# A hybrid encoder layer on one core: the second attention branch loads split queries, keys and masked biases instead of raw ones

## The chip, the cores and the metric

The kernel runs on one core of a Trainium2 chip. The metric is the device time of one execution in microseconds (us). TensorE (PE) multiplies matrices into PSUM, with its weight loads (PEld) beside it; VectorE (DVE), ScalarE (ACT) and GpSimd (POOL) work element by element; SyncE (SP) issues most DMAs.

## What is computed

A sandwich-normalised encoder layer on 1024 sample and 256 prompt positions of width 1024, each a request of its own:

```python
h = rms_norm(x, pre_mix_norm)
qa, ka, va, qb, kb, vb, g_a, g_b = jnp.split(h @ w_in, SPLIT_POINTS, axis=-1)
o_a = gqa_branch(qa, ka, va, q_norm, k_norm) @ w_proj_a      # 8 query heads, 2 kv heads of 64
o_b = neighbourhood_branch(qb, kb, vb, rpb) @ w_proj_b       # 8 heads of 64
mix = (sigmoid(g_a + b) * o_a + sigmoid(g_b + b) * o_b) @ w_out
x = x + rms_norm(mix, post_mix_norm)
# channel mixer: up-projection, depthwise conv of 3, gelu(gate) * value, down-projection, norm, add
```

In the neighbourhood branch the positions are a grid of rows of 64 columns. A query sees 8 rows of 16 columns, each score gets a bias from a table of 15 x 31 per head (`rpb`), and the rest of the row is masked with minus infinity:

```python
s = einsum('bqhd,bwkhd->bhqwk', q_row, k_band) * scale + bias
s = where(col_mask, s, -inf); p = softmax(s, axis=(-2, -1))
```

All is float32. TensorE multiplies in a reduced form, so each operand x is held as two halves, hi = x rounded to that form and lo = x - hi, and a product takes two or three matmuls.

## The kernel before, in words

Splitting is a helper, `split_hi_lo` (L67): ScalarE casts hi (L68), VectorE subtracts lo (L69). A framework orders the instructions of each engine by a simulated timeline, in about the order in which the code states them, and sets the semaphores; `issue_after` and `behind` pin an instruction behind another on its engine. Each engine, SP's DMA queue too, then works in that fixed order.

1. First projections (to 178 us): for ten tiles of 128 positions the queries and keys of branch A with norms and rotary embedding (`project`, `rope`, `rope_t`). `rope_t` transposes and ScalarE copies the queries into the SBUF tile `qT` (L271). A second loop (L338) gives the values of both branches; between its steps `bias_tables` (L322) builds in DRAM the padded tables `rp_d` and `gv_d` of the relative bias, and the values of branch B go to DRAM by 64 stores (L355, on SP and ScalarE).

2. Branch A (178 to some 498 us): eight heads of five blocks of 256 queries. `Pipe.unit` interleaves the scores of a block with the transposes of the block before it and the outputs of the one before that. `q_stack` (L149) splits the queries of a head out of `qT`, two blocks ahead. At the second head the table `rq_d` for the prompt bias is written (L525). Softmax is a maximum on VectorE (L489), an exponential on ScalarE (L451), a reciprocal on VectorE (L453) and a normalisation on GpSimd (L454); the transposed probabilities are split (L68, L69).

3. Beside this, TensorE is filled with the rest of the projection (`fill_units`, L380): 24 blocks of 128 columns of `w_in`, 4 for the queries of branch B, 4 for its keys, 16 for the gates, each in three chunks of 512, 512 and 256 positions. A chunk is 24 matmuls (L395 to L397) in 8 units into one PSUM bank, `fp`, with `bufs=1`; then ScalarE copies the bank to the tile `fo`, scaling queries (L401), and SP stores it to `qb_d`, `kb_d` or `g_d` (L402). `fill_plan` and `fill` spread the units over the blocks: 216 of 576 in branch A, 32 at its end, up to 544 in branch B, the rest after. The 24 chunks of queries and keys are the first 192 units.

4. Branch B (some 500 to 780 us): eight heads of five blocks, four of 16 columns of the grid and one prompt block. `prep` (L555) loads the raw queries and keys of the next head, the bias `g16` in eight DMAs (L567), the values and the prompt bias `gp`; then, a step at a time between the blocks, ScalarE and VectorE split the keys (L589) and the queries, put into block order (L592 to L596), and GpSimd adds the row mask to the bias (L600) and the column mask to the prompt bias (L604). Scores: two matmuls (L620, L621), then one VectorE instruction that adds the bias and takes the maximum (L624). `sum_halves` (L456) adds the two halves of an output: ScalarE L458, VectorE L465, GpSimd L466.

5. From some 800 us: output projections, mix, and the channel mixer to 1893 us.

Of the kernel before, what the change touches and what calls it, by code (L numbers as in the profile page):

```python
# [16 lines left out]
P = 128  # L17
# [22 lines left out]
def encoder_layer_kernel(  # L40
# [52 lines left out]
    qb_d = scratch("qb_d", [4, P, NT])  # L93
    kb_d = scratch("kb_d", [4, P, NT])
# [8 lines left out]
    gv_d = scratch("gv_d", [NH, 16, 3, 23, 32])  # L103

# [40 lines left out]
    qT = T(av, "qT", [P, 4, NT])  # L145
    kH = T(av, "kH", [P, 2, NT], F32R)
    kL = T(av, "kL", [P, 2, NT], F32R)

    def q_stack(h):  # L149
        qs = T(qsp[0], "qs", [P, NT], F32R, bufs=2)  # L150
        a = slice((h % 2) * HD, (h % 2) * HD + HD)
        b = slice((1 - h % 2) * HD, (1 - h % 2) * HD + HD)
        src = qT[a, h // 2, :]
        nc.scalar.copy(qs[a, :], src)
        nc.vector.tensor_sub(qs[b, :], src, f32(qs[a, :]))
        return qs

    qsp = [None]
    qs_next = {}

    with ExitStack() as st:
# [104 lines left out]
        def rope_t(tt, qr, kr):  # L266
# [4 lines left out]
            nc.scalar.copy(qT[:, :, cols], tq)  # L271
# [44 lines left out]
        nc.sync.dma_start(rpad[:, 16:47], rpb[0].rearrange("h d c -> d h c"))  # L316
        bm = T(spv, "bm", [P, 3, 32])
# [4 lines left out]
        def bias_tables(step):  # L322
            if step == 1:
# [3 lines left out]
                nc.sync.dma_start(rp_d[15 * NH * 992:15 * NH * 992 + 32], rpad[0:1, 0:32])  # L327
            elif step == 3:
# [50 lines left out]

    def fill_units():  # L380
        for blk in range(24):
            if blk < 8:
                c0 = 768 + blk * P
                dst = (qb_d if blk < 4 else kb_d)[blk % 4]
                scale = QSCALE if blk < 4 else 1.0
            else:
                c0 = 2304 + (blk - 8) * P
                dst = g_d[blk - 8]
                scale = 1.0
            hi, lo = stream_w([(slice(0, NK), w_cols(w_in, c0))], () if blk else [fill_state["dve"].ins])  # L390
            for (t0, n) in CHUNKS:
# [8 lines left out]
                fo = T(stream, "fo", [P, 512], bufs=2)  # L400
                nc.scalar.activation(fo[:, 0:n], fp[:, 0:n], AF.Copy, scale=scale)  # L401
                nc.sync.dma_start(dst[:, t0:t0 + n], fo[:, 0:n])  # L402
# [68 lines left out]
    with va_stack:  # L471
        with ExitStack() as st:
# [45 lines left out]
            rpad2 = T(sp, "rpad2", [NH * 7, 127])  # L518
            nc.gpsimd.memset(rpad2, 0.0)
            nc.sync.dma_start(rpad2[:, 48:79], rpb[0][:, 4:11, :])  # L520

            pipe = Pipe()
            for h in range(NH):
                if h == 1:
                    nc.sync.dma_start(rq_d, rpad2.unsqueeze(1).to_broadcast([NH * 7, GW, 127]))  # L525
                qs = qs_next.pop(h)
                for j in range(5):
# [10 lines left out]
    with ExitStack() as st:  # L538
# [4 lines left out]
        cm = T(sp, "cm", [P, GW])  # L543
        nc.sync.dma_start(cm, col_mask)
        rm = T(sp, "rm", [P, 2, 12])
        nc.sync.dma_start(rm, row_mask)

        def by_block(ap, reverse):
            step = ap.ap[-1][0]
            first, dr = (15 * GW, -GW) if reverse else (0, 16)  # L550
            db = 16 if reverse else 256
            return bass.AP(tensor=ap.tensor, offset=ap.offset + first * step,
                           ap=[list(ap.ap[0]), [db * step, 4], [dr * step, 16], [step, 16]])

        def prep(h, res):  # L555
            pr, r0 = h // 2, (h % 2) * HD
            qraw = T(sp, "qraw", [HD, NT], bufs=1)
            nc.sync.dma_start(qraw, qb_d[pr, r0:r0 + HD, :])
            kraw = T(sp, "kraw", [P, NT], bufs=1)
            for half in range(2):  # L560
                nc.sync.dma_start(kraw[half * HD:(half + 1) * HD, :], kb_d[pr, r0:r0 + HD, :])
            g16 = T(sp, "g16", [P, 3, 16, 32], bufs=1)
            gt = gv_d[h]
            for r8 in range(8):
                src = bass.AP(tensor=gt.tensor, offset=gt.offset + r8 * 32,
                              ap=[[3 * 23 * 32, 16], [23 * 32, 3], [1, 512]])
                nc.sync.dma_start(g16[r8 * 16:(r8 + 1) * 16].rearrange("p v a b -> p v (a b)"), src)  # L567
# [4 lines left out]
            gp = T(sp, "gp", [P, 6, GW], bufs=2)  # L572
            rq = rq_d[h * 7:h * 7 + 1]
            for half in range(2):
                src = bass.AP(tensor=rq.tensor, offset=rq.offset + (1 - half) * GW * 127 + 63,
                              ap=[[126, GW], [GW * 127, 6], [1, GW]])
                nc.sync.dma_start(gp[half * GW:(half + 1) * GW], src)
            qs = T(sp, "qs", [P, NT], F32R, bufs=2)
            kh = T(sp, "kh", [P, NT], F32R, bufs=2)
            kl = T(sp, "kl", [P, NT], F32R, bufs=2)  # L580
            gb = T(sp, "gb", [P, 2, 3, 12, 32], bufs=2)
            ost = T(sp, "ost", [HD, NT], bufs=1)
            res.extend((gb, gp, qs, kh, kl, vB, ost))
            yield
# [90 lines left out]
        for _ in prep(0, cur):  # L675
            pass
# [644 lines left out]
```

## Time and profile before

| | us |
|---|---|
| median of 3 runs (lowest to highest) | 1897.12 (1894.83 to 1897.34) |
| the profiled execution | 1895.24 |
| its span, first to last instruction | 1893.5 |
| TensorE busy, of that span | 1841.7 (97%) |
| VectorE, ScalarE, GpSimd busy | 1253.2, 862.7, 673.7 |
| TensorE's mean granted clock | 0.993 |

The profile is of one execution. Busy time of a matmul is modelled to its end, so a busy TensorE need not be at its peak. A row of a timeline gives start and duration in us, the engine, the line of the kernel, the operation, output<-inputs, the shape and a count; in brackets stands how long the engine was idle before it and which instruction ended that. A row by stage gives for each engine the busy us and (x) the instructions, then the granted clock as a share of full speed, the mean busy share of the 16 DMA engines, and GB/s.

### The profile page before, as it was taken

The page shows a single profiled execution, that of the slowest core. Times are in us where ns is not written, and L with a number is a line of the kernel's source. Part 1 is how long each engine was busy: PE and PEld are TensorE (multiplying, and loading weights), DVE is VectorE, ACT ScalarE, POOL GpSimd, SP SyncE. Part 2 cuts the span into 40 slices and gives each one's busy share as a digit, 9 for nine tenths or more (in the row PEclk, how much of TensorE's full clock was granted, in tenths as well). Part 3 has the DMA queues.
Part 4 walks back from the last instruction along what each step waited for, and adds up shares of the span by engine and source line. Part 5 has one row for each costly group of instructions (what it writes and reads, how often), then busy time and mean ns, then how long its engine had stood idle before and what let it go on. Part 6 is the DMA issues. An engine that isn't in the chain of part 4 may idle for free.

```text
span 1893.5 us, 27341 instructions
## 1 busy us (share of the span) xinstructions
PE 1841.7 (97%) x10048; PEld 1590.3 (84%) x10048; DVE 1253.2 (66%) x1872; ACT 862.7 (46%) x1535; POOL 673.7 (36%) x609
## 2 busy tenths in 40 slices
PE   7999999999989999999999999999999999899998
PEld 7998888888778888888888888888888888778886
DVE  6844667667456766355644778877777776768775
ACT  4322667566446555444432434444444443553332
POOL 3731322222155544102111355543334432166531
PEclk9999999999989999999999999999999999999999
DMA  5146411111485663364532212322222223798865
GB/s 192 34 110 204 82 37 47 44 40 48 116 192 159 161 157 107 94 209 149 187 120 91 69 63 79 102 93 79 76 80 94 91 86 107 257 307 268 268 208 178
DMA packets 237352, 240.74 MB, mean 127 GB/s; under 512 B 32737, under 2 KB 183201, under 8 KB 237089
## 3 DMA queue, kind: packets, MB, share of 16 engines
q1 hardware_dynamic: 235537, 234.52, 41.3%
q10 hardware_dynamic: 1680, 4.46, 0.7%
q8 instruction: 79, 1.29, 0.3%
q14 instruction: 56, 0.46, 0.1%
HBM read 169.38 MB, written 69.55 MB: 126 GB/s over the span
## 4 chain that ended last, share of the span: by engine, by line
PE 63%; DVE 3%; DMA 2%; issue 2%; POOL 1%; ACT 1%; DVEq 0%; POOLq 0%; ACTq 0%; SPq 0%
PE pp L804 10%; PE pp L805 10%; PE pp L803 10%; PE big L744 5%; PE sml L805 3%; PE sml L804 3%; PE sml L803 3%; PE fp L395 2%; PE fp L396 2%; PE fp L397 2%; PE big L767 2%; PE big L765 2%; PE big L766 2%; DMA wr<-in_w_down_dram 2%; PE sml L744 1%
## 5 line engine op out<-in xcount | busy, mean ns | idle before, releaser
L454 POOL TENSOR_SCALAR p<-p,rs 128x384 f32<-128x384 f32 (+2 forms) x160 | 130.4, 818 | 303.4 <-DVE rs L453 259.2
L395 PE MATMUL fp<-bigH,fh 128*128 128x512 f32 (+1 forms) x544 | 207.7, 382 | 6.3 <-ACT fo L401 5.3
L397 PE MATMUL fp<-bigH,fl 128*128 128x512 f32 (+1 forms) x544 | 195.9, 360 | 0.5 <-DVE fl L69 0.5
L396 PE MATMUL fp<-bigL,fh 128*128 128x512 f32 (+1 forms) x544 | 196.0, 360 | 0.0
L804 PE MATMUL pp<-bigL,th 128*128 128x512 f32 (+1 forms) x556 | 192.4, 346 | 0.0
L803 PE MATMUL pp<-bigH,th 128*128 128x512 f32 (+1 forms) x556 | 191.9, 346 | 0.0
L805 PE MATMUL pp<-bigH,tl 128*128 128x512 f32 (+1 forms) x556 | 190.7, 346 | 0.0
L1115 POOL TENSOR_TENSOR wt<-wr,wr 128x512 f32<-128x512 f32 x55 | 99.6, 1836 | 84.1 <-DVE m L69 52.7
L69 DVE TENSOR_TENSOR ptL<-t,ptH 128x512 fp32r<-128x512 f32 x144 | 93.9, 657 | 50.6 <-ACT ptH L68 50.3
L395 PEld LDWEIGHTS fp<-bigH,fh 128*128 128x128 f32 x544 | 103.6, 190 | 21.1 <-ACT fo L401 7.3
L397 PEld LDWEIGHTS fp<-bigH,fl 128*128 128x128 f32 x544 | 103.3, 190 | 17.2 <-DVE fl L69 1.0
L803 PEld LDWEIGHTS pp<-bigH,th 128*128 128x128 f32 x556 | 104.6, 188 | 15.1
L805 PEld LDWEIGHTS pp<-bigH,tl 128*128 128x128 f32 x556 | 104.6, 188 | 14.9
L804 PEld LDWEIGHTS pp<-bigL,th 128*128 128x128 f32 x556 | 104.6, 188 | 14.6
L68 ACT CAST ptH<-t 128x512 fp32r<-128x512 f32 x144 | 80.4, 564 | 75.1 <-PE t L506 73.4
L396 PEld LDWEIGHTS fp<-bigL,fh 128*128 128x128 f32 x544 | 103.9, 191 | 11.9
L489 DVE TENSOR_REDUCE nm<-s 128x1 f32<-128x1024 f32 (+1 forms) x80 | 84.8, 1060 | 17.7 <-PE s L487 17.4
L805 PE MATMUL pp<-m,shl 128*128 128x512 f32 x242 | 94.2, 389 | 0.0
L803 PE MATMUL pp<-m,shl 128*128 128x512 f32 x242 | 94.2, 389 | 0.0
L804 PE MATMUL pp<-m,shl 128*128 128x512 f32 x242 | 94.2, 389 | 0.0
L1067 POOL TENSOR_TENSOR ss<-f,f 128x640 f32<-128x640 f32 x33 | 59.8, 1840 | 92.9 <-DVE f L906 47.1
L69 DVE TENSOR_TENSOR tl<-ts,th 128x512 fp32r<-128x512 f32 x76 | 63.3, 833 | 38.1 <-ACT th L68 37.9
(327 smaller groups left out, 5370.9 us busy)
## 6 DMA issues: line engine op xcount, KB each, us to landing
wr<-in_w_down_dram SPq DMA_DIRECT2D x132, 256.0 KB, 4.8
sr<-s_d SPq DMA_DIRECT2D x30, 704.0 KB, 6.2
s_d<-ss SPq DMA_DIRECT2D x55, 320.0 KB, 2.9
fraw<-in_w_in_dram SPq DMA_DIRECT2D x24, 512.0 KB, 4.0
wg<-in_w_up_dram SPq DMA_DIRECT2D x22, 512.0 KB, 3.8
wv<-in_w_up_dram SPq DMA_DIRECT2D x22, 512.0 KB, 4.2
g<-g_d SPq DMA_DIRECT2D x16, 640.0 KB, 4.8
g_d<-fo SPq DMA_DIRECT2D x32, 256.0 KB, 4.3
```

The source lines that it names most:

```text
L68: nc.scalar.copy(hi, src)
L69: nc.vector.tensor_sub(lo, src, f32(hi))
L395: nc.tensor.matmul(o, hi[:, k, :], bigH[:, k, t0:t0 + n], start=(k == 0), stop=False)
L396: nc.tensor.matmul(o, hi[:, k, :], bigL[:, k, t0:t0 + n], start=False, stop=False)
L397: nc.tensor.matmul(o, lo[:, k, :], bigH[:, k, t0:t0 + n], start=False, stop=(k == NK - 1))
L454: nc.gpsimd.tensor_scalar(p[:, 0:n], p[:, 0:n], rs, 1.0, op0=ALU.mult, op1=ALU.mult)
L489: fill_state["dve"] = nc.vector.tensor_reduce(nm, s[:, 0:nkey], axis=AX.X, op=ALU.max, negate=True)
L744: nc.tensor.matmul(outs[c], w[:, 4 * br + k, :], o[br][k][:, t0:t0 + n], start=(k == 0 and w is wh and o is oH), stop=(k == 3 and w is wl))
L803: nc.tensor.matmul(o, wh, mh, start=first, stop=False, skip_group_check=True)
L804: nc.tensor.matmul(o, wh, ml, start=False, stop=False, skip_group_check=True)
L805: return nc.tensor.matmul(o, wl, mh, start=False, stop=last, skip_group_check=True)
L1115: (nc.gpsimd.tensor_add if spec[1][2] > 0 else nc.gpsimd.tensor_sub)(src, raws[0], raws[1])
```

## The change

Queries and keys of branch B are split where they leave the projection, and both halves go to DRAM (`store_qk`); the scale of the scores goes from the queries to the keys, and the queries are put into block order on the way. The biases are masked in branch A by `bias_of`, a step after each block, and go to DRAM finished. Branch B loads finished operands: `operands` of the next head at its second block and `values` at its third. `rq_d` is written in step 2 of `bias_tables`. The queries of branch A no longer stay in `qT`: they are stored to `q_d` and loaded a head at a time (`q_load`).

```diff
@@ rope_t
-            nc.scalar.copy(qT[:, :, cols], tq)
+            qt = T(sp, "qt", [P, 4, P], bufs=2)
+            nc.scalar.copy(qt, tq)
+            nc.sync.dma_start(q_d[:, :, cols].rearrange("g p c -> p g c"), qt)
@@ q_load, q_stack
+    def q_load(h):
+        q_raw[h] = T(qsp[0], "qraw", [HD, NT], bufs=1)
+        nc.sync.dma_start(q_raw[h], q_d[h // 2, (h % 2) * HD:(h % 2 + 1) * HD, :])
...
-        src = qT[a, h // 2, :]
+        src = q_raw.pop(h)
@@ bias_tables, loop over the values
+            elif step == 2:
+                nc.sync.dma_start(rq_d, rpad2.unsqueeze(1).to_broadcast([NH * 7, GW, 127]))
...
+            if tt == 2:
+                q_load(0)
@@ fill_units
+    def store_qk(blk, t0, n, src):
+        if (3 * blk + t0 // 512) % 2:
+            parts = [T(stream, "fo", [P, 512], F32R, bufs=2) for _ in range(2)]
+        else:
+            both = T(qk_sp[0], "qk", [P, 2, 512], F32R, bufs=1)
+            parts = [both[:, 0, :], both[:, 1, :]]
+        hi, lo = (t[:, 0:n] for t in parts)
+        if blk >= 4:
+            nc.scalar.activation(hi, src, AF.Copy, scale=QSCALE)
+            nc.vector.scalar_tensor_tensor(lo, src, QSCALE, f32(hi), op0=ALU.mult, op1=ALU.subtract)
+            for x in range(2):
+                nc.sync.dma_start(kb_d[blk - 4, x, :, t0:t0 + n], f32((hi, lo)[x]))
+            return
+        if t0 < NS:
+            src = bass.AP(tensor=src.tensor, offset=src.offset + 7 * GW * src.ap[-1][0],
+                          ap=[list(src.ap[0]), [16, 4], [-GW, 8], [1, 16]])
+            split_hi_lo(*(t.rearrange("p (b r c) -> p b r c", b=4, c=16) for t in (hi, lo)), src)
+        else:
+            split_hi_lo(hi, lo, src)
+        for x in range(2):
...
+            nc.sync.dma_start(dst, part)
@@ branch A
+            def bias_of(h):
+                g16 = T(sp, "g16", [P, 3, 16, 32], bufs=1)
...
+                for r8 in range(8):
...
+                    if r8 % 4 == 3:
+                        yield
+                gp = T(sp, "gp", [P, 6, GW], bufs=1)
...
+                for i in range(2):
+                    gb = T(sp, "gb", [P, 3, 12, 32], bufs=1)
+                    for v in range(3):
+                        nc.gpsimd.tensor_add(gb[:, v], g16[:, v, 4 * i:4 * i + 12, :],
+                                             rm[:, i, :].unsqueeze(2).to_broadcast([P, 12, 32]))
+                    nc.sync.dma_start(gb_d[h, :, i], gb)
+                    yield
+                nc.gpsimd.tensor_add(gp, gp, cm.unsqueeze(1).to_broadcast([P, 6, GW]))
+                nc.sync.dma_start(gp_d[h], gp)
+                yield
...
                     pipe.unit(stage1(h, qs, j, pts), stage2(h, j, pts))
+                    next(bias)
+                    if j == 0 and h + 1 < NH:
+                        q_load(h + 1)
@@ branch B, in place of prep
+        def operands(h):
+            pr, rows = h // 2, slice((h % 2) * HD, (h % 2 + 1) * HD)
+            qs = T(sp, "qs", [P, NT], F32R, bufs=2)
+            kh = T(sp, "kh", [P, NT], F32R, bufs=2)
+            kl = T(sp, "kl", [P, NT], F32R, bufs=2)
             for half in range(2):
+                at = slice(half * HD, (half + 1) * HD)
+                nc.sync.dma_start(f32(kh[at, :]), kb_d[pr, 0, rows, :])
+                nc.sync.dma_start(f32(qs[at, :]), qb_d[pr, half, rows, :])
+                nc.sync.dma_start(f32(kl[at, :]), kb_d[pr, 1, rows, :])
+            gb = T(sp, "gb", [P, 2, 3, 12, 32], bufs=2)
+            nc.sync.dma_start(gb, gb_d[h])
+            gp = T(sp, "gp", [P, 6, GW], bufs=2)
+            nc.sync.dma_start(gp, gp_d[h])
+            return gb, gp, qs, kh, kl
...
-                if cb >= 1:
-                    steps(preps)
...
+                if h + 1 < NH and cb == 1:
+                    nxt = operands(h + 1)
+                if h + 1 < NH and cb == 2:
+                    nxt = nxt + values(h + 1)
```

## Rows read from the trace of the kernel before

**Rows 1.** By stage: branch A, then branch B in two parts, and all from the end of branch A to the end of the projection. Columns: stage, its us, then busy us (x instructions) of PE, PEld, DVE, ACT and POOL, granted clock, DMA share, GB/s.

```profile
178.00:490.00 312.00, 307.51 (x1950) 271.34 (x1950) 216.13 (x365) 199.34 (x391) 82.15 (x80) 1.00 0.20 52
515.00:560.00 45.00, 35.74 (x179) 29.46 (x179) 26.12 (x79) 19.80 (x50) 26.84 (x33) 0.89 0.96 217
560.00:780.00 220.00, 212.09 (x1235) 185.96 (x1234) 143.14 (x423) 121.44 (x299) 102.31 (x131) 0.99 0.52 137
490.00:822.00 332.00, 312.75 (x1784) 271.28 (x1783) 193.96 (x541) 171.38 (x400) 131.96 (x169) 0.98 0.60 158
```

**Rows 2.** Timeline of TensorE from 499 to 822 us: nine of the larger waits, by the matmul or transpose that ended them.

```profile
517.29 0.45 PE L620 MATMUL s<-kh,qs 128*128 128x384 f32 x1 [1.00 <-DVE mx L624]
519.66 0.44 PE L620 MATMUL s<-kh,qs 128*128 128x384 f32 x1 [1.74 <-DVE mx L624]
...
542.45 0.58 PE L663 MATMUL pv<-pt,vB 128*128 128x256 f32 x1 [2.96 <-DVE pt L69]
543.68 0.90 PE L650 MATMUL t<-ident,p 128*128 128x128 f32 x3 [0.43 <-POOL p L454]
548.79 0.79 PE L395 MATMUL fp<-bigH,fh 128*128 128x512 f32 x1 [2.93 <-ACT fo L401]
592.07 0.50 PE L395 MATMUL fp<-bigH,fh 128*128 128x512 f32 x1 [1.21 <-ACT fo L401]
...
631.36 0.55 PE L650 MATMUL t<-ident,p 128*128 128x128 f32 x3 [1.93 <-POOL p L454]
...
698.47 0.55 PE L650 MATMUL t<-ident,p 128*128 128x128 f32 x3 [2.55 <-POOL p L454]
723.78 0.55 PE L650 MATMUL t<-ident,p 128*128 128x128 f32 x3 [0.82 <-POOL p L454]
```

**Rows 3.** Timeline of GpSimd and VectorE in the same stage: preparation that waited for a DMA.

```profile
515.81 4.77 POOL L600 TENSOR_TENSOR gb<-g,rm 128x384 f32<-128x384 f32 x6 [25.68 <-DMA g<-gv_d]
537.40 3.20 POOL L600 TENSOR_TENSOR gb<-g,rm 128x384 f32<-128x384 f32 x4 [9.31 <-DMA vB<-vp_d]
541.17 0.76 DVE L592 TENSOR_TENSOR qs<-qraw 64x512 fp32r<-64x512 f32 x1 [4.15 <-DMA qraw<-qb_d]
695.62 1.00 POOL L604 TENSOR_TENSOR gp<-gp,cm 128x384 f32<-128x384 f32 x1 [5.50 <-DMA gp<-rq_d]
```

**Rows 4.** Two stretches of 5 us, the end of the waits at 542 to 549 us and what follows; columns as in rows 1.

```profile
545.00:550.00 5.00, 2.07 (x8) 1.48 (x7) 3.55 (x8) 4.33 (x11) 0.83 (x2) 0.50 1.06 254
550.00:555.00 5.00, 5.00 (x19) 3.92 (x18) 3.81 (x13) 1.26 (x4) 3.24 (x5) 0.76 0.98 233
```

**Rows 5.** Groups by line from 490 to 822 us, the larger part of the work of `prep`. Columns: line, engine, operation, out<-in, shapes, count, then busy us, mean ns of one, idle us before it and what ended it.

```profile
L600 POOL TENSOR_TENSOR gb<-g,rm 128x384 f32<-128x384 f32 x48 | 50.5, 1084 | 59.2 <-DMA g<-gv_d 25.7 <-DVE mx L624 14.4 <-DMA vB<-vp_d 9.3
L69 DVE TENSOR_TENSOR kl<-kraw,kh 128x512 fp32r<-128x512 f32 (+1 forms) x24 | 18.6, 798 | 3.5 <-ACT kh L68 3.3
L592 DVE TENSOR_TENSOR qs<-qraw 64x512 fp32r<-64x512 f32 x16 | 14.9, 945 | 11.4 <-DMA qraw<-qb_d 11.4
L593 DVE TENSOR_TENSOR qs<-qraw,qs 64x512 fp32r<-64x512 f32 x16 | 14.5, 911 | 0.3
L604 POOL TENSOR_TENSOR gp<-gp,cm 128x384 f32<-128x384 f32 x8 | 9.0, 1123 | 16.9 <-DMA gp<-rq_d 16.1 <-DVE pt L69 0.7
```

**Rows 6.** Groups by line from 178 to 490 us, columns as in rows 5, and one row of the view of line 69 there (count: shortest/median/longest ns, first and last start in us, forms).

```profile
L489 DVE TENSOR_REDUCE nm<-s 128x1 f32<-128x1024 f32 (+1 forms) x80 | 84.8, 1060 | 17.7 <-PE s L487 17.4
L454 POOL TENSOR_SCALAR p<-p,rs 128x1024 f32<-128x1024 f32 (+1 forms) x80 | 82.3, 1029 | 256.7 <-DVE rs L453 215.9 <-PE t L506 27.7 <-PE s L487 7.1
L401 ACT ACTIVATE fo<-fp 128x512 f32<-128x512 f32 (+1 forms) x26 | 13.9, 535 | 3.0 <-PE fp L397 2.7
...
L69 DVE TENSOR_TENSOR ptL<-t,ptH x138: 409/691/694, 188.8 to 488.7; 128x512 fp32r<-128x512 f32 x124, 128x256 fp32r<-128x256 f32 x14
```

**Rows 7.** Timeline of branch A: ScalarE's copy out of the projection's bank and the first matmul of the next chunk, for the first and the last of the 24 chunks of queries and keys.

```profile
195.94 0.59 ACT L401 ACTIVATE fo<-fp 128x512 f32<-128x512 f32 x1
199.56 0.39 PE L395 MATMUL fp<-bigH,fh 128*128 128x512 f32 x1
...
466.68 0.40 ACT L401 ACTIVATE fo<-fp 128x256 f32<-128x256 f32 x1
468.01 0.48 PE L395 MATMUL fp<-bigH,fh 128*128 128x512 f32 x1
```

**Rows 8.** DMA issues from 500 to 780 us, one of its rows: out<-in, queue, operation, count, size of one, median us from issue to landing.

```profile
qraw<-qb_d SPq DMA_DIRECT2D x8, 320.0 KB, 5.0
```

**Rows 9.** The view of line 600 and that of line 155 (columns as the last of rows 6), and from the timeline the GpSimd addition beside which the first of line 155 ran.

```profile
L600 POOL TENSOR_TENSOR gb<-g,rm x48: 825/835/2290, 515.8 to 719.7; 128x384 f32<-128x384 f32 x48
L155 DVE TENSOR_TENSOR qs<-qT,qs x8: 1485/1487/4883, 147.5 to 443.1; 64x1280 fp32r<-64x1280 f32 x8
146.03 4.96 POOL L334 TENSOR_TENSOR gv<-gv,bm 128x2208 f32<-128x2208 f32 x1 [29.17 <-DMA vw_d<-vs]
```

**Rows 10.** The issue of the table `rq_d` in the timeline, and stretches of the values' projection and of the start of branch A, columns as in rows 1.

```profile
183.29 0.86 SPq L525 DMA_DIRECT2D rq_d<-rpad  x1
125.00:175.00 50.00, 50.00 (x341) 50.00 (x342) 13.32 (x25) 7.86 (x22) 5.10 (x2) 1.00 0.75 204
180.00:185.00 5.00, 2.74 (x10) 1.64 (x10) 5.00 (x8) 3.38 (x6) 0.00 (x0) 1.00 0.32 118
190.00:200.00 10.00, 10.00 (x61) 8.72 (x60) 7.20 (x12) 6.46 (x13) 3.47 (x4) 1.00 1.12 120
```

More of the change, by code (lines that the diff above doesn't have):

```diff
@@ L316, in encoder_layer_kernel @@
         nc.sync.dma_start(rpad[:, 16:47], rpb[0].rearrange("h d c -> d h c"))
+        rpad2 = T(spv, "rpad2", [NH * 7, 127])
+        nc.gpsimd.memset(rpad2, 0.0)
+        nc.sync.dma_start(rpad2[:, 48:79], rpb[0][:, 4:11, :])
         bm = T(spv, "bm", [P, 3, 32])
@@ L399, in fill_units @@
                         yield 1
-                fo = T(stream, "fo", [P, 512], bufs=2)
-                nc.scalar.activation(fo[:, 0:n], fp[:, 0:n], AF.Copy, scale=scale)
-                nc.sync.dma_start(dst[:, t0:t0 + n], fo[:, 0:n])
+                if blk < 8:
+                    store_qk(blk, t0, n, fp[:, 0:n])
+                else:
+                    fo = T(stream, "fo", [P, 512], bufs=2)
+                    nc.scalar.copy(fo[:, 0:n], fp[:, 0:n])
+                    nc.sync.dma_start(g_d[blk - 8][:, t0:t0 + n], fo[:, 0:n])
                 yield 2
@@ L516, in stage2 @@
                 nc.sync.dma_start(o_d[0, h // 2, (h % 2) * HD:(h % 2 + 1) * HD, j * 256:(j + 1) * 256], o)
-            rpad2 = T(sp, "rpad2", [NH * 7, 127])
-            nc.gpsimd.memset(rpad2, 0.0)
-            nc.sync.dma_start(rpad2[:, 48:79], rpb[0][:, 4:11, :])
+            cm = T(sp, "cm", [P, GW])
+            nc.sync.dma_start(cm, col_mask)
+            rm = T(sp, "rm", [P, 2, 12])
+            nc.sync.dma_start(rm, row_mask)
+            qk_sp[0] = sp
+            def bias_of(h):
+                g16 = T(sp, "g16", [P, 3, 16, 32], bufs=1)
+                gt = gv_d[h]
+                for r8 in range(8):
+                    src = bass.AP(tensor=gt.tensor, offset=gt.offset + r8 * 32,
+                                  ap=[[3 * 23 * 32, 16], [23 * 32, 3], [1, 512]])
+                    nc.sync.dma_start(g16[r8 * 16:(r8 + 1) * 16].rearrange("p v a b -> p v (a b)"), src)
+                    if r8 % 4 == 3:
+                        yield
+                gp = T(sp, "gp", [P, 6, GW], bufs=1)
+                rq = rq_d[h * 7:h * 7 + 1]
+                for half in range(2):
+                    src = bass.AP(tensor=rq.tensor, offset=rq.offset + (1 - half) * GW * 127 + 63,
+                                  ap=[[126, GW], [GW * 127, 6], [1, GW]])
+                    nc.sync.dma_start(gp[half * GW:(half + 1) * GW], src)
+                for i in range(2):
[8 more added lines that the diff above has]
+                yield
             pipe = Pipe()
             for h in range(NH):
-                if h == 1:
-                    nc.sync.dma_start(rq_d, rpad2.unsqueeze(1).to_broadcast([NH * 7, GW, 127]))
                 qs = qs_next.pop(h)
+                bias = bias_of(h)
                 for j in range(5):
@@ L541, in encoder_layer_kernel, with values @@
         fill_plan(B_FILL, 200)
[L543 to L559, printed above, removed]
-            for half in range(2):
[L561 to L567, printed above, removed]
+        def operands(h):
[3 more added lines that the diff above has]
+            kl = T(sp, "kl", [P, NT], F32R, bufs=2)
+            for half in range(2):
+                at = slice(half * HD, (half + 1) * HD)
[7 more added lines that the diff above has]
+            return gb, gp, qs, kh, kl
+        def values(h):
             vB = T(sp, "vB", [P, 18, P], F32R, bufs=2)
@@ L571, in prep @@
                 nc.sync.dma_start(f32(vB[:, 16 + t, :]), vp_d[:, t, h, :])
[L572 to L584, printed above, removed]
[L585 to L605 removed]
+            return vB, T(sp, "ost", [HD, NT], bufs=2)
         def stage1(bufs, cb, out):
@@ L673, in encoder_layer_kernel @@
         pipe = Pipe()
-        cur = []
-        for _ in prep(0, cur):
-            pass
-        preps = None
+        cur = operands(0) + values(0)
         for h in range(NH):
```

53 lines of the change are left out of this document (13 added, 40 removed).

## The prediction

> **What bounds the kernel now.** I read the table by stage first [rows 1]. From 178 to 490 us (the first attention branch) TensorE is busy for 307.5 of 312 us: it is the bound there, and 2.26 of its 4.5 idle us lie between 180 and 185 us [rows 10]. From 490 to 822 us (the second branch, then the projections left over) it is busy for 312.75 of 332 us: 19.25 us are lost, 9.3 of them in 515 to 560 us, where the DMA engines' share is 0.96 and the granted clock averages 0.89. VectorE, ScalarE and GpSimd are far from full in both stages; what they do late costs only where TensorE then stands still.
>
> The second view is the timeline of TensorE in that stage, for the pieces with idle time before them [rows 2]. The nine larger ones shown hold 15.6 of the 19.25 us; the others are waits of at most 0.7 us. Behind them stands the preparation of the next head. At 517 and 519 us the scores wait for VectorE's maximum, whose bias is added only from 515.81 us on, when its DMA is there [rows 3]. At 542 to 549 us VectorE stood 4.15 us for the raw query, with the split of the probabilities and its own half of the keys' split queued behind; GpSimd had waited 9.31 us with the bias additions and did six in a row, and ScalarE's copy that frees the projection's PSUM bank came late. At 698 us TensorE waits for a normalisation that stood on GpSimd behind the prompt bias, and that behind 5.50 us of a DMA [rows 3]; the wait at 631 us is of the same kind. So TensorE waits here for work that is not late by itself but stands in an engine's order behind a wait for a DMA.
>
> At the end of the waits at 542 to 549 us the granted clock is 0.50, in the 5 us after them 0.76 [rows 4]; 0.50 is the lower of its two levels, 1.2 GHz. In the first stretch 2.07 us of work ran at half speed, in the second 5.0 us at 0.76.
>
> **The change, part by part.** TensorE gets the same matmuls and transposes; none is added. The time moves by what TensorE waits.
>
> *Preparation leaves the second branch.* By line this is 14.9 + 14.5 us on VectorE for the query, 18.6 for the keys' low half, and 50.5 + 9.0 on GpSimd [rows 5], with the smaller casts some 15 us of ScalarE besides; a head has 33 us. With it go its waits for DMAs. Gain: of the waits shown the seven from 542 us on, 2.96 + 0.43 + 2.93 + 1.21 + 1.93 + 2.55 + 0.82 = 12.8 us [rows 2]. The two at 517 and 519 us (2.74) belong to head 0, whose operands cannot land before the first branch has freed their places: I take half, 1.4. The slower clock gives back 2.07 x 0.5 + 5.0 x 0.24, so some 2.0 us [rows 4]. Together 16; with all of head 0's and the small waits 20; with half the waits staying for other reasons 8. What is late next is the single bank for the projection: ScalarE's copy is queued behind others, and waits of 0.2 to 0.7 us for it stay.
>
> *The split at the projection.* The first 24 chunks (blocks 0 to 7, three each) all fall in the first branch. Each had one ScalarE copy out of the bank; now a copy of the same size and a VectorE subtraction that reads the bank too. ScalarE's work stays what it was, 0.54 us a chunk on the mean [rows 6]. VectorE gets 16 x 0.69 + 8 x 0.41, 14 us, in 312 us where it works 216 [rows 1, 6]: room enough in sum. But there is one bank (bufs=1), and TensorE's next chunk now waits for both readers. Between the end of ScalarE's copy and the next chunk's first matmul the 24 gaps average 1.26 us, five of them under 0.45; the first and the last are shown, 3.0 and 0.9 us [rows 7]. If VectorE takes the subtraction w us after the copy ends, a chunk loses 0.69 (0.42 for 256 columns) + w less its gap. Summed over the 24 gaps that is 2 us for w = 0.05, 6 for w = 0.5 and 14.5 for w = 1.1, one maximum of 1.06 us standing ahead [rows 6]. VectorE is free three tenths of the time, so w lies between; the order of the instructions may also move the next chunk back. I take 5; ends 2 and 14.5. The 24 extra stores have until the second branch to land.
>
> *Bias additions in the first branch.* 56 GpSimd additions, 59.5 us [rows 5], join 82.3 us of normalisations [rows 6] in 312 us. A normalisation can come behind one addition, 0.83 us [rows 9]. TensorE never waited for GpSimd there, since a block's transposes are issued one block (7.8 us) later; if a third of the 56 delays by 0.5 us got through it were 9 us. I take 1; ends 0 and 9. Their loads and stores are queued on SP between weights and outputs; DMA share there is 0.20 [rows 1], and a weight block is fetched one block ahead.
>
> *The table rq_d moves* from the first branch to the values' projection. It was issued at 183.29 us, and from 190 to 200 us the DMA share is 1.12 at 120 GB/s [rows 10]: 1.8 MB, some 14 us of all 16 engines. From 125 to 175 us the share is 0.75 [rows 10], so 12.5 us are free for 14, and the first query's load of 320 KB stands on SP's queue behind it, as do the value stores. VectorE and ScalarE are nearly idle there (13.3 and 7.9 of 50 us), so a late store is first met by idle engines; on the other side TensorE's 2.26 us of waiting at 180 to 185 us may shrink. I take 1 lost; ends -2 and 10.
>
> *The query through DRAM.* Ten stores and eight loads of 320 KB replace an SBUF tile. A load is asked for two blocks (15 us) ahead of the split; its like landed in 5.0 us [rows 8]. Nothing, unless SP stands at another wait for 10 us.
>
> *Loads in the second branch.* A head fetched 3.1 MB: query 0.33, keys 0.66, bias 0.79 and 0.2, values 1.18. Now six half tiles of 0.33, the finished bias 1.18 + 0.2, values 1.18: 4.5 MB. At 217 GB/s, the rate where the engines are full [rows 1], this is 21 us of 33, beside some 2 MB of weights and gate rows a head (9 us). It fits, asked for at the second block, three blocks ahead. I take 1 lost; ends 0 and 8.
>
> Sum: -16 + 5 + 1 + 1 + 1 = -8 us, against the profiled execution's 1895.24 us, whose span is 1893.5. The median of the runs shown, 1897.12, is 1.9 above that execution: 1897.1 - 8 = **1889**.
>
> **Rivals.** *The bank is held too long* (slower). The place is the single bank in the first branch, where TensorE has nothing in reserve. For it: VectorE is 69% busy with pieces of 0.69 and 1.06 us in order, and a chunk that finds a low half and a maximum ahead waits w = 1.8, for which the 24 gaps give 28 us: -16 + 28 + 2 = +14, **1911**. It decides from w = 1.1 on, where the gain is used up. Against it: VectorE would have to be behind at nearly every chunk. A second delay has its row: a subtraction on VectorE of two SBUF operands took 4.88 us instead of 1.49 when a GpSimd addition of 4.96 us had begun 1.5 us before it [rows 9], ending about 1.4 us after it; so each of the 27 such pieces in the first branch (20 low halves of weights, 7 of queries) can be held by up to 0.83 us by an addition. By "SBUF — State Buffer" of the Trainium skill ("SBUF: two separate sides") the two engines' shared port pair is taken whole for an instruction; the trace's 4.88 us agrees, and by that rule subtractions out of PSUM with one SBUF input, the new ones among them, would not be held.
>
> *The DMA engines fill up in the values' projection.* For it: 14 us into 12.5 free, with value stores behind it on the same queue. If the first weights and the last stores come 8 us late, TensorE stands that long at 178 to 190 us: -8 + 8 - 1, about **1896**, no change.
>
> *The loads come late in the second branch.* For it: the share of 0.96 at 515 to 560 us, where two heads' loads meet. One us lost for each head: -8 + 7, **1896**. Against it: the large transfers now are rows of 5 and 9 KB, and no engine's order waits in the middle of other work for them.
>
> *The bank costs nothing*, since the order of instructions makes room: -20 + 2 = **1879**.
>
> **How the numbers follow.** A measurement of this kernel can tell about 0.2% (3.8 us) from no change. Forecast (a gain of 4 to 14 us): 0.50. Bank free of cost: 0.10. Late loads: 0.11, half of it still over 3.8 us faster. Full DMA engines: 0.13, mostly no change. Bank held: 0.16, most of it slower. Faster: 0.50 + 0.10 + 0.06 = 0.66. Same 0.17, slower 0.17. The range takes the gain of 20 with costs of 0 at one end, 1877; at the other the costs of 8 + 14.5 - 5 against 12.8, that is +5, 1902.
>
> **What would show it.** In the profile after: GpSimd's and VectorE's busy time in the second branch down by some 60 and 50 us; no wait of GpSimd for a DMA there; TensorE's idle time in 490 to 822 us near 5 us in place of 19, with a granted clock at 1.00. In the first branch TensorE's waits for the projection's bank would appear with VectorE named: 5 us in all. It is wrong if those waits reach 14 us, if TensorE stands for over 5 us more at 175 to 190 us, or if scores in the second branch wait for operands at each head's first block.

## The result, and the profile after

The changed kernel takes 1921.62 us (median; 1919.75 to 1922.59) against 1896.44 us of the kernel before: a ratio of 1.0133 [1.0121, 1.0145]. It is slower by some 25 us, where 1889 us was predicted with 1877 to 1902 us as the range. The profiled execution took 1920.9 us with a span of 1919.1 us, 25.6 more than the span before; all that follows splits these 25.6 us.

The same piece of work exists in both traces, so the delay can be read along the way: the start of ScalarE's copy of the n-th output block of branch A, after minus before.

| point | delay, us | since the point above |
|---|---|---|
| first block of branch A | 13.3 | +13.3 |
| last block of its fourth head | 32.6 | +19.3 |
| last block of branch A | 37.5 | +4.9 |
| last copy of the projection (end of branch B) | 19.8 | -17.7 |
| end of the span | 25.6 | +5.8 |

So branch B did gain what was forecast, 17.7 us against 16. Everything in front of it lost, and a little behind it. By stage (columns as in [rows 1]), cut so that the stretches of the two kernels hold the same matmuls to within one: the kernel before, branch A and branch B to the end of the projection; then the kernel after, the same two stages, and the passage from the output projections to the channel mixer.

```profile
178.00:500.00 322.00, 316.85 (x2025) 280.14 (x2024) 221.42 (x375) 204.66 (x403) 82.29 (x80) 1.00 0.20 52
500.00:821.00 321.00, 302.41 (x1702) 261.65 (x1703) 187.77 (x531) 165.71 (x388) 131.82 (x168) 0.98 0.61 161
```

```profile
180.00:537.00 357.00, 326.64 (x2024) 285.82 (x2023) 235.59 (x401) 203.90 (x405) 127.03 (x136) 0.96 0.42 124
538.00:841.00 303.00, 295.03 (x1702) 258.19 (x1701) 137.79 (x467) 153.90 (x356) 69.11 (x112) 0.99 0.74 211
1030.00:1080.00 50.00, 47.13 (x216) 38.83 (x215) 20.90 (x20) 13.25 (x24) 10.65 (x19) 0.97 0.20 74
```

TensorE stands 30.4 us in branch A instead of 5.2, at a mean clock of 0.96 instead of 1.00; in branch B it stands 8.0 instead of 18.6, GpSimd has 63 us less work there and VectorE 50 less. Its busy time in branch B falls too, by 7.4 us for the same 1702 matmuls.

**Branch B** goes as described ahead. The waits for the preparation of [rows 2] and [rows 3] are gone; GpSimd waits for no DMA any more (its two groups below, columns as in [rows 5], against L600 and L604 there, which are gone). The two larger waits of TensorE that remain are the first head's operands and, as forecast, ScalarE's late copy of the bank:

```profile
L495 POOL TENSOR_SCALAR p<-p,rs 128x384 f32<-128x384 f32 (+1 forms) x80 | 45.7, 576 | 88.2 <-DVE rs L494 58.3 <-DVE nm L657 29.4
L507 POOL TENSOR_TENSOR ost<-otmp 64x256 f32<-64x256 f32 x32 | 23.5, 735 | 125.1 <-DVE nm L657 66.5 <-DVE otmp L506 54.6 <-DVE rs L494 4.0
```

```profile
552.61 0.80 PE L652 MATMUL s<-kl,qs 128*128 128x384 f32 x3 [1.59 <-DMA kl<-kb_d]
567.71 0.50 PE L433 MATMUL fp<-bigH,fh 128*128 128x512 f32 x1 [3.10 <-ACT fo L442]
```

**The start.** The timeline of the kernel after, from the issue of `rq_d` in the values' projection to the first scores:

```profile
137.25 0.90 SPq L339 DMA_DIRECT2D rq_d<-rpad  x1
138.19 9.34 SPq L153 DMA_DIRECT2D qraw<-q_d  x1
138.88 17.20 ACTq L369 DMA_DIRECT2D vw_d<-vs  x4
156.12 0.27 ACT L68 CAST vA<-pj 128x128 fp32r<-128x128 f32 x1 [18.09 <-DMA qraw<-q_d]
187.08 0.76 PE L527 MATMUL s<-kH,qs 128*128 128x512 f32 x1 [6.19 <-DVE vs L69]
194.27 0.79 PE L433 MATMUL fp<-bigH,fh 128*128 128x512 f32 x1 [5.15 <-ACT fh L68]
```

The issue of `rq_d` itself is short (0.90 us). The next transfer on SP takes 9.34 us to issue, and four value stores that ScalarE issues take 17.20 us. ScalarE's own work is in the same order behind them: it stands 18.09 us. The delay reaches TensorE 30 us later, as 6.19 us for the last values and 5.15 us for the first weights.

**The first heads of branch A.** Here the masked bias of the second branch is on GpSimd, three additions (L584) at a time, with TensorE's waits among them:

```profile
240.57 2.41 POOL L584 TENSOR_TENSOR gb<-g,rm 128x384 f32<-128x384 f32 x3 [9.59 <-DMA gp<-rq_d]
242.94 0.99 POOL L588 TENSOR_TENSOR gp<-gp,cm 128x384 f32<-128x384 f32 x1
243.91 2.21 POOL L495 TENSOR_SCALAR p<-p,rs 128x1024 f32<-128x1024 f32 x2
245.08 1.12 PE L547 MATMUL t<-ident,p 128*128 128x128 f32 x4 [3.74 <-POOL p L495]
...
319.54 1.12 PE L547 MATMUL t<-ident,p 128*128 128x128 f32 x4 [3.52 <-POOL p L495]
332.89 2.42 POOL L584 TENSOR_TENSOR gb<-g,rm 128x384 f32<-128x384 f32 x3 [7.42 <-DMA qb_d<-qk]
336.45 0.66 PE L547 MATMUL t<-ident,p 128*128 128x128 f32 x4 [1.95 <-POOL p L495]
```

The code states one step of `bias_of` after each block, so that the eight heads' tables would be spread over branch A. The framework's order has all 48 additions of L584 between 201.9 and 341 us, in the first four heads. The groups wait for DMAs, up to 9.59 us: gathers of their tables, or stores that free their single buffers. A softmax normalisation (L495) stands behind each group in the order, and TensorE's transposes then stand for the normalisation. From 200 to 345 us GpSimd waits 60 us for DMAs in front of additions.

### The profile page after: what moved, and what is told of

It is laid out like the page before. It is cut to its first block, busy times and chain, and to the rows that moved or that the text cites. A ratio compares the mean times of both kernels' runs of the same rounds, so it can differ in the third digit from the quotient of the medians.

```text
span 1919.1 us, 27467 instructions
## 1 busy us (share of the span) xinstructions
PE 1847.4 (96%) x10048; PEld 1594.3 (83%) x10048; DVE 1218.5 (63%) x1832; ACT 847.7 (44%) x1503; POOL 655.1 (34%) x609
## 5 line engine op out<-in xcount | busy, mean ns | idle before, releaser
L495 POOL TENSOR_SCALAR p<-p,rs 128x384 f32<-128x384 f32 (+2 forms) x160 | 125.3, 788 | 256.8 <-DVE rs L494 205.3
L547 PE MATMUL t<-ident,p 128*128 128x128 f32 x544 | 83.6, 276 | 10.7 <-POOL p L495 10.4
```

Of the source, the lines that this page charges most:

```text
L495: nc.gpsimd.tensor_scalar(p[:, 0:n], p[:, 0:n], rs, 1.0, op0=ALU.mult, op1=ALU.mult)
L547: fill_state["pe"] = nc.tensor.transpose(tp[:, a, :], pts[i][:, (g + a) * P:(g + a + 1) * P], ident)
```

## The experiments

Three rounds each, five for `copy_bank`, with the kernel before run beside them. "A grows by" is the delay at the last block of branch A less that at its first; "B" the change from there to the projection's last copy; "tail" the rest of the span; all of the profiled executions, against the same trace of before.

| kernel | median, us | ratio, 95% interval | start | A grows by | B | tail |
|---|---|---|---|---|---|---|
| the change | 1921.62 | 1.0133 [1.0121, 1.0145] | 13.3 | 24.2 | -17.7 | 5.8 |
| spread | 1904.37 | 1.0044 [1.0031, 1.0057] | 14.3 | 8.4 | -16.8 | 5.8 |
| rq_alone | 1905.47 | 1.0052 [1.0034, 1.0070] | 10.2 | 0.1 | -1.7 | 2.0 |
| q_alone | 1895.20 | 0.9991 [0.9979, 1.0003] | 3.4 | -0.1 | -2.9 | 1.1 |
| both | 1894.87 | 0.9997 [0.9985, 1.0009] | 0.6 | 8.4 | -17.7 | 6.5 |
| bias_q | 1880.35 | 0.9914 [0.9899, 0.9928] | 0.9 | 1.0 | -17.8 | 1.0 |
| split_q | 1900.77 | 1.0020 [1.0011, 1.0029] | 3.1 | 8.5 | -8.1 | 0.6 |
| both_copy | 1886.21 | 0.9948 [0.9931, 0.9964] | 1.9 | 1.3 | -19.8 | 3.5 |
| both_bank | 1890.02 | 0.9965 [0.9952, 0.9978] | 4.3 | 8.5 | -17.9 | 0.6 |
| copy_bank | 1882.54 | 0.9936 [0.9923, 0.9950] | 3.9 | 1.1 | -17.7 | -1.5 |
| rq_pieces | 1918.40 | 1.0118 [1.0101, 1.0135] | 23.3 | 0.1 | 0.8 | -0.2 |
| rq_act | 1901.13 | 1.0033 [1.0023, 1.0042] | 6.4 | 0.1 | -3.1 | 0.5 |

The column "start" is uncertain by some 4 us: `both` and `both_bank` are the same program up to the channel mixer and show 0.6 and 4.3.

### Which part lost what

**spread**: the changed kernel with each bias step held behind the normalisation that stands in front of it in the code.

```diff
                     pipe.unit(stage1(h, qs, j, pts), stage2(h, j, pts))
-                    next(bias)
+                    with behind(ENG_POOL):
+                        next(bias)
```

> The changed kernel with one edit: each step of the bias work is pinned on GpSimd behind the normalisation of the block after which the code states it. In the changed kernel's trace the 48 mask additions of all eight heads run from 202 to 343 us, inside the first four heads of the first branch, beside a DMA share of 0.64, and the delay against the kernel before grows from 13.3 us (head 0, block 3) to 32.6 us (head 3). Theory (run ahead by the scheduler, the additions wait on GpSimd for crowded DMAs and hold normalisations): spread over eight heads most of these 19 us go, total 1903 to 1908 us, and the delay from head 0 to head 3 is under 5 us. Rival (the additions cost GpSimd's time wherever they stand): no gain, 1917 to 1925 us, with the delay growing evenly over the heads.

17 us of the 25 go. The same work on the same engine, only in its stated place: A grows by 8.4 in place of 24.2, so 15.8 us were the order. Two stretches of the kernel after, then the same two of this one (columns as in [rows 1]):

```profile
235.00:250.00 15.00, 11.26 (x50) 9.38 (x49) 6.49 (x14) 5.46 (x13) 9.43 (x11) 0.80 0.64 180
295.00:345.00 50.00, 43.38 (x260) 37.49 (x260) 31.35 (x53) 25.88 (x52) 28.16 (x31) 0.97 0.54 165
```

```profile
235.00:250.00 15.00, 14.91 (x85) 12.54 (x84) 11.39 (x21) 10.05 (x22) 5.29 (x4) 1.00 0.39 104
295.00:345.00 50.00, 48.13 (x325) 43.30 (x324) 38.24 (x64) 34.24 (x68) 21.56 (x23) 1.00 0.47 129
```

From 200 to 345 us TensorE stands 13.2 us in the one and 3.6 in the other; the lower clock (0.80 on 11.3 us of work, 0.97 on 43.4) costs some 3.6 more, an estimate. GpSimd waits 60 us for DMAs in front of additions there; here not one of the 56 additions waits, since they come late enough to find their tables landed.

**rq_alone**: the kernel before, with only the write of `rq_d` moved into the values' projection.

```diff
+            elif step == 2:
+                nc.sync.dma_start(rq_d, rpad2.unsqueeze(1).to_broadcast([NH * 7, GW, 127]))
...
-                if h == 1:
-                    nc.sync.dma_start(rq_d, rpad2.unsqueeze(1).to_broadcast([NH * 7, GW, 127]))
```

> The kernel before with one part of the change: the prompt bias table is written in step 2 of the values' projection (with its padded source tile), all else as before. Theory (this write of 1.8 MB in rows of 508 bytes fills the DMA queue and holds value stores, evacuation and the first weights): the first branch's outputs are about 13 us late, total 1905 to 1911 us. Rival (the query's way through DRAM, with ScalarE standing for the load, makes the late start): within 3 us of the kernel before.

9.6 us lost, all of it ahead of branch A's first block (10.2) and constant through it. The first query's load, absent here, accounts for at most the 3 us more of the whole change, and these lie within the uncertainty of that column.

**q_alone**: the kernel before, with only the queries of branch A stored to `q_d` and loaded by head (`q_load`).

> The kernel before with another part of the change: the queries of the first branch go through DRAM and are loaded a head at a time; the table is written where it was. Theory (the table's write makes the late start): within 3 us of the kernel before, 1894 to 1900 us. Rival (the load of the first query, for which ScalarE stands in the values' projection, makes it): 1905 to 1911 us.

No difference that can be measured, as forecast.

**both**: the changed kernel with the bias steps held in place and `rq_d` written at the start of branch A instead.

```diff
-            elif step == 2:
-                nc.sync.dma_start(rq_d, rpad2.unsqueeze(1).to_broadcast([NH * 7, GW, 127]))
...
+            nc.sync.dma_start(rq_d, rpad2.unsqueeze(1).to_broadcast([NH * 7, GW, 127]))
             qk_sp[0] = sp
```

> The changed kernel with the bias steps pinned as in the run spread, and the prompt bias table written at the start of the first branch in place of step 2 of the values' projection. Theory (two causes that add): 17 us from the pins and 13 us from the table, 1888 to 1897 us, and the gain of 17 us in the second branch stays. Rival (the split at the projection costs the first branch as much by its one bank): not under 1905 us.

The two corrections bring the loss to nothing, but not to the forecast gain: A still grows by 8.4 us, and the tail by 6.5.

### Where the rest goes

My theory for the 8.4 us was the additions themselves, beside the normalisations. Two kernels take the halves of the change apart. Both start from the kernel before with the queries of branch A through DRAM (which makes the room in SBUF).

**bias_q**: of the change only the masked tables, with both corrections: `bias_of` held in place, `rq_d` at the start of branch A, `gb` and `gp` loaded in branch B, which still splits its queries and keys.

> Kernel before, with the queries of the first branch through DRAM (which cost nothing by itself) and of the change only the masked bias tables: rq_d written at the start of branch A, the bias steps kept at their places in GpSimd's order, branch B loading the two finished tables and still splitting its own queries and keys. Theory (what is left of A's loss, 9 us at its end in the kernel with both corrections, lies with the additions on GpSimd, in front of the softmax's normalisation): A's end 7 to 9 us late, B shorter by 4 to 8 since GpSimd leaves its preparation, 1896 to 1902 us. Rival (the loss lies with the split at the bank): A's end at most 3 us late, 1888 to 1893 us.

**split_q**: of the change only `store_qk`, the split at the bank, and the loads of the split halves; the biases are gathered and masked in branch B as before.

> The other half: kernel before with the queries of the first branch through DRAM, and of the change only the split of branch B's queries and keys at the projection's bank; the bias tables are still gathered and masked in branch B. Theory (loss with the additions): A's end at most 3 us late, B shorter by 8 to 13, 1884 to 1889 us. Rival (loss with the split): A's end 6 to 9 us late, 1890 to 1895 us.

The theory fell, and both times lie outside what was expected of either side. The tables alone leave branch A as it was (+1.0) and give branch B its whole gain (-17.8): 1880 us, the best kernel of the study. The split alone costs branch A 8.5 us and gives branch B 8.1. The two gains don't add, since 17.8 and 8.1 make 17.7 to 19.8 together: once GpSimd's waits are gone branch B is bound by TensorE's work (295 of 303 us in the kernel after), and what the split would take away is no longer on the path.

**both_copy**: `both`, where ScalarE copies the bank to SBUF first, and both halves are made from the copy.

```diff
-        if (3 * blk + t0 // 512) % 2:
-            parts = [T(stream, "fo", [P, 512], F32R, bufs=2) for _ in range(2)]
-        else:
-            both = T(qk_sp[0], "qk", [P, 2, 512], F32R, bufs=1)
-            parts = [both[:, 0, :], both[:, 1, :]]
+        parts = [T(stream, "fo", [P, 512], F32R, bufs=2) for _ in range(2)]
         hi, lo = (t[:, 0:n] for t in parts)
+        raw = T(qk_sp[0], "qkraw", [P, 512], bufs=1)[:, 0:n]
+        nc.scalar.copy(raw, src)
+        src = raw
```

> The kernel with both corrections, where ScalarE first copies the bank to SBUF and both parts are made from the copy: the bank is free after one copy, as before the change, and ScalarE has one instruction more per chunk. If the hold of the bank costs in A: the two waits of 0.5 to 0.8 us on the low part go, and A's end comes 1 to 3 us earlier, 1892 to 1894 us. If the load of ScalarE and VectorE costs: A's end 2 to 5 us later, 1897 to 1900 us. If neither: 1894 to 1896 us.

ScalarE gets 24 instructions more and the loss goes: A grows by 1.3, and the kernel is faster than any of the three expectations said (1892 us at best). So it was the bank, held until VectorE had read it, and not the work. Nor was it the places for the halves, which this kernel allots otherwise too: in `both` neither ScalarE nor VectorE waits for a store of a half in branch A. One chunk of `both` in the timeline, and the same chunk of `both_copy`; first its last matmul, then its readers, then the next chunk:

```profile
400.90 0.28 PE L430 MATMUL fp<-bigH,fl 128*128 128x256 f32 x1
402.44 0.38 ACT L397 ACTIVATE fo<-fp 128x256 fp32r<-128x256 f32 x1
402.74 1.22 DVE L525 TENSOR_REDUCE nm<-s 128x1 f32<-128x1024 f32 x1
403.88 0.98 DVE L69 TENSOR_TENSOR fl<-fraw,fh 128x512 fp32r<-128x512 f32 x1
404.78 0.41 DVE L398 SCALAR_TENSOR_TENSOR fo<-fp,fo 128x256 fp32r<-128x256 f32 x1
405.15 0.39 PE L522 MATMUL s<-kH,qs 128*128 128x256 f32 x1 [1.36 <-ACT p L487]
405.50 0.40 PE L428 MATMUL fp<-bigH,fh 128*128 128x512 f32 x1
```

```profile
398.41 0.28 PE L429 MATMUL fp<-bigH,fl 128*128 128x256 f32 x1
399.89 0.38 ACT L393 COPY qkraw<-fp 128x256 f32<-128x256 f32 x1
401.08 0.48 PE L427 MATMUL fp<-bigH,fh 128*128 128x512 f32 x1
```

In `both` VectorE's subtraction comes 1.96 us after ScalarE's half has ended, behind a maximum and half a weight's split, and the bank is held for 4.0 us. This is one of the late ones: over the 24 chunks of queries and keys that delay runs from 0.03 to 2.54 us, 0.68 on the mean, and the time from a chunk's last matmul to the end of its last reader is 1.39 us on the mean before, 2.62 in `both`, 1.39 in `both_copy`. Only 1.6 us of TensorE's waits for the bank in branch A name VectorE's low half. The larger ones name something else, as the wait at 405.15 does: while the bank is held no projection matmul can run, the order goes on through the score and transpose matmuls it has, and then stands for ScalarE's exponential. These are the rows that name it among TensorE's waits from 160 to 520 us (us in total, times, longest), in `both` and in `both_copy`:

```profile
PE s L522 <- ACT p L487: 4.9, 7, 1.4
```

```profile
PE s L521 <- ACT p L486: 0.9, 1, 0.9
```

**both_bank**: `both`, with the channel mixer's rotation of PSUM banks begun at bank 2.

```diff
-    banks = [0]
+    banks = [2]
```

> The kernel with both corrections, and the channel mixer's rotation of PSUM banks begins at bank 2 in place of 0, nothing else. Theory (the mixer's first accumulation falls on the PSUM slot that the last output projection's VectorE addition still reads; TensorE waits 2.9 us there and then runs 3 to 4 us at 1.2 GHz): the tail is 4 to 5 us shorter and the time 1889 to 1891 us. Rival (the wait is for the data and only named by the slot): 1894 to 1896 us, with the wait on another line.

4.85 us less, as expected. The first accumulation of the channel mixer in the kernel after, in `both`, and in `both_bank`:

```profile
1070.03 0.68 PE L825 MATMUL pp<-bigH,th 128*128 128x512 f32 x1 [2.87 <-DVE oraw L796]
```

```profile
1041.69 0.48 PE L826 MATMUL pp<-bigH,th 128*128 128x512 f32 x1 [2.86 <-DVE oraw L797]
```

```profile
1042.12 0.47 PE L826 MATMUL pp<-bigH,th 128*128 128x512 f32 x1
```

No line of the change is there. TensorE waits for VectorE's scaling of the output projection's last tile, and the wait goes when the rotation begins two banks on: so that tile, one of three that rotate in PSUM, lay where the mixer's first bank is. The granted clock is lower behind the wait, 0.83 from 1070 to 1080 us in the kernel after. Why the tiles fell otherwise than in the kernel before was not traced; `bias_q` and `split_q`, with one half of the change each, have no such wait.

**copy_bank** (five rounds): the four corrections together.

> All four corrections of the change together: rq_d at the start of branch A, the bias steps kept at their places, the bank copied once before the split, the channel mixer's rotation begun at bank 2. If the terms are independent: the kernel with the copy less the 4.7 to 4.9 us that the rotation gave, 1880 to 1883 us, so no better than the bias tables alone (1880) and the split worth nothing. If the shorter branch B moves the output projection so that the slot of its last tile is another: 1885 to 1888 us.

1882.54 us, as the sum of the terms said: 0.6% faster than before, and no faster than the tables alone (1880.35). Made without its losses, the split at the projection is worth nothing that these runs can show.

### Why the table costs where it is written

**rq_pieces**: as `rq_alone`, but in eight writes, one in each of the steps 2 to 9. **rq_act**: as `rq_alone`, with ScalarE issuing the write.

```diff
+            if 2 <= step < 10:
+                r7 = slice((step - 2) * 7, (step - 1) * 7)
+                nc.sync.dma_start(rq_d[r7], rpad2[r7].unsqueeze(1).to_broadcast([7, GW, 127]))
```

```diff
-                nc.sync.dma_start(rq_d, rpad2.unsqueeze(1).to_broadcast([NH * 7, GW, 127]))
+                nc.scalar.dma_start(rq_d, rpad2.unsqueeze(1).to_broadcast([NH * 7, GW, 127]))
```

> Kernel before with rq_d written in the values' projection on SP's queue, but in eight pieces of 448 rows, one in each of the steps 2 to 9, the same bytes in all. If what costs is the one long write at the head of SP's queue (stores and loads behind it stand for 9 to 18 us): each piece holds the queue some 2 us, branch A starts at most 4 us late, 1895 to 1900 us. If what costs is that the stage's 16 DMA engines are full with 1.8 MB more: as with the one write, 9 to 11 us late, 1904 to 1907 us.

> The same write in one piece in step 2, but issued by ScalarE, whose queue carries a quarter of the stage's transfers; SP's queue is free of it. If the place in SP's queue costs: the loads of the masks and of the first weights are on time, branch A starts at most 4 us late, 1895 to 1900 us; if the DMA engines are full, or ScalarE then stands at its own stores in the same way: 8 to 12 us late, 1903 to 1908 us.

Neither expectation for the pieces held: 23.3 us late, for the same bytes that cost 10.2 in one write. The order on SP shows why: six of the eight pieces were run ahead and stand in a row. Timeline of `rq_pieces`:

```profile
156.12 16.24 SPq L328 DMA_DIRECT2D rq_d<-rpad  x6
158.74 23.21 ACTq L361 DMA_DIRECT2D vw_d<-vs  x4
181.99 0.27 ACT L68 CAST vA<-pj 128x128 fp32r<-128x128 f32 x1 [24.78 <-DMA rq_d<-rpad]
184.45 0.60 PE L232 MATMUL pj<-wh,bigH 128*128 128x320 f32 x1 [13.70 <-DVE vs L69]
```

SP takes 16.24 us to issue six, and meanwhile ScalarE, on its own queue, needs 23.21 us to issue four stores (1.88 to 6.85 us for four in the kernel before, the longest just behind the write of `rp_d`). Its copies out of PSUM wait behind these, all the projection's banks stay full, and TensorE stands for 13.70 us. With ScalarE issuing the one write branch A starts 6.4 us late (1901.13 us, in between the two expectations): there too its next four stores took 20.71 us.

```profile
127.40 20.71 ACTq L360 DMA_DIRECT2D vw_d<-vs  x4
148.15 0.27 ACT L68 CAST vA<-tp 128x128 fp32r<-128x128 f32 x1 [23.39 <-DMA vw_d<-vs]
```

So the number of bytes doesn't set the price: 0.6 to 4.3 us in the five kernels that write at the start of branch A, no more than the column is uncertain by, and 6.4, 10.2 and 23.3 us in the values' projection by how the writes fall. While such a write runs, issuing takes long. The kernel before has it too, behind its write at 183.29 us [rows 10]; the first weights of branch A were already loaded and split by then, and TensorE shows no wait for the next ones:

```profile
184.27 12.34 SPq L365 DMA_DIRECT2D fraw<-in_w_in_dram  x2
```

In the kernel after, in `rq_pieces` and in `rq_act` the delay enters where ScalarE's order holds issues of its own. In `rq_alone` ScalarE stood 21.0 us as well, but the trace names the gather on SP behind the write. How the issuing of one queue comes to be held by the other's transfers was not isolated.

## Why the prediction was wrong

- *Preparation leaves the second branch*, 16 us: right in path and in sum, 17.7 measured. That the sum came so near is in part luck: of it 14.2 were to be idle time and 2.0 the clock, and 10.6 us of idle time went and 7.4 of TensorE's busy time. The clock gives some 2.8 of these: 0.61 on 7.2 us of work and 0.76 on 5.5 before (540 to 553 and 697 to 704 us), 0.79 on 6.3 after (566 to 574 us), an estimate. Where the rest of the 7.4 comes from stays open. What the halves showed is that the tables alone bring the gain.
- *Bias additions in the first branch*, 1 us with ends 0 and 9: this step failed. 15.8 us by `spread`, and with the additions where the code puts them 1.0 (`bias_q`), which is what the step had priced. It took the place in the code for the place in the order. Nothing tied a bias step to its block, the framework ordered by its own timeline, and the additions moved to where their data were not. Then not one addition of 0.83 us stands in front of a normalisation, but a DMA wait of up to 9.59 us with three or four additions behind it, 12.99 us in all in the row shown, more than the one block of 7.8 us that covers it.
- *The table rq_d moves*, 1 us with ends -2 and 10: failed too, 10 us alone and 13 with the query's load behind it, a difference that the measurement can't tell from none. The 14 us of transfers against 12.5 free were counted, and "a late store is first met by idle engines" was wrong: half of the sample tiles' value stores are issued by ScalarE, whose order also holds the copies out of PSUM. The rival of the full DMA engines named this term, at 8 us. The sign given for it, over 5 us more of standing at 175 to 190 us, was not reached: TensorE stands 7.2 us there instead of 3.4, and the wait of 5.15 us at 194 us lies outside the stretch.
- *The split at the projection*, 5 us with ends 2 and 14.5: right in kind, 8.4 measured. w came to 0.68 us on the mean, for which, held constant, the prediction's own reckoning over the 24 gaps gives 8.3; the 5 taken stands for too small a w. The sign to look for was badly chosen, though: waits that name VectorE at the bank make up 1.6 us, the others are shifted to score matmuls.
- *The query through DRAM*, 0: right (0.9991). *Loads in the second branch*, 1: 1.6 us of waiting for the first head's keys, 0.2 for its values, nothing later.
- Not in the sum at all: 5.8 us behind the change, 4.9 of them one PSUM slot by `both_bank`.
- *The range*: its slow end, 1902, let only the split go to its end. The ends given for the additions and for the table, 9 and 10, are not in it, and both terms reached or passed them.

The terms measured are -17.7 + 15.8 + 13.3 + 8.4 + 5.8 = 25.6 us. The rival with the bank held too long gave the sign and came nearest, at 1911 us, but by luck: its term was a third of the 28 us it was given. The two that decided were held to be worth 1 us each, and both errors are of one kind: the work was priced, and not what it stands in front of when its data are late.

## What to carry to other kernels

Moving work from a stage that waits into one where TensorE has no slack paid here only where every moved instruction came to stand behind its data: pin it behind the instruction it is meant to follow, and look at the order that results before counting its duration. A single PSUM bank was priced here by its last reader, not by the work; one copy that freed it was cheaper than two readers. Before two savings are added, ask whether they end the same wait: here the half that was left alone gave all of it.

## What the runs showed of the hardware

A subtraction with one PSUM operand kept its time where one with two SBUF operands was slower, beside GpSimd's additions and normalisations. The same low half of a key chunk, read from the bank in `both` and from the SBUF copy in `both_copy` (200 to 500 us, columns as in [rows 5]):

```profile
L398 DVE SCALAR_TENSOR_TENSOR fo<-fp,fo 128x512 fp32r<-128x512 f32 x4 | 2.7, 679 | 1.3 <-ACT fo L397 1.3
```

```profile
L397 DVE SCALAR_TENSOR_TENSOR fo<-qkraw,fo 128x512 fp32r<-128x512 f32 x8 | 6.1, 763 | 2.0 <-ACT fo L396 2.0
```

679 ns from PSUM, 763 from SBUF. The second mean is made by a few: of 128x512 elements, with nothing of GpSimd beside it, either kind takes 670 to 695 ns. Six of the 24 subtractions in `both_copy` began while a GpSimd instruction was running, and all but the one that began 0.08 us before its end were longer (861 to 1334 ns); in `both` ten of 24 did, and none was longer. One of each, `both_copy` first:

```profile
355.72 1.14 POOL L489 TENSOR_SCALAR p<-p,rs 128x1024 f32<-128x1024 f32 x1 [4.30 <-DVE rs L488]
356.06 1.33 DVE L397 SCALAR_TENSOR_TENSOR fo<-qkraw,fo 128x512 fp32r<-128x512 f32 x1
```

```profile
377.49 1.01 POOL L588 TENSOR_TENSOR gp<-gp,cm 128x384 f32<-128x384 f32 x1
378.15 0.69 DVE L398 SCALAR_TENSOR_TENSOR fo<-fp,fo 128x512 fp32r<-128x512 f32 x1 [1.26 <-ACT fo L397]
```

That is in keeping with the rule of "SBUF — State Buffer" in the Trainium skill ("SBUF: two separate sides") weighed ahead: the shared port pair holds up VectorE's instructions with two SBUF inputs, and not these. The price was small here, since `both_copy` is the faster by 8.7 us all the same.

Issuing was the other surprise: an issue that takes 0.5 to 1.7 us on ScalarE's queue in the kernel before took 4 to 6 us while `rq_d` was being written from SP's (17.20 us for four in the kernel after, 23.21 in `rq_pieces`).
